# Moving GpSimd's share of the lo parts, quarters and sums of squares to VectorE, and starting the feed-forward with four weight groups

## The chip, the core and the metric

One core of a Trainium2 chip runs the whole program. The metric is device time in microseconds (us) of one execution; lower is better. The engines are TensorE (PE, with its weight loads PEld), VectorE (DVE), ScalarE (ACT), GpSimd (POOL) and SyncE (SP, which issues most transfers).

## The reference, cut to what matters

Two layers of a decoder over 1024 tokens with 1024 features. Every product is in float32.

```python
for i in range(DEPTH):                                   # 2
    proj = rmsnorm(h, attn_norm_g[i]) @ w_in[i]          # split into four head groups
    y_a = mla_group(...)      # 4 heads, causal softmax attention
    y_b = fox_group(...)      # 4 heads, causal softmax attention with a forgetting bias
    y_c = hgrn2_group(...)    # gated linear recurrence
    y_d = s5_group(...)       # complex-diagonal state space
    h = h + concat(rmsnorm of each, y_c gated) @ w_out[i]
    h = h + conv_ffn(rmsnorm(h, ffn_norm_g[i]), w_up[i], conv_w[i], conv_b[i], w_down[i])
    h = h + sigmoid(rmsnorm(h, ple_norm_g[i]) @ w_ple_gate[i]) * (p[i] @ w_ple[i])
return rmsnorm(h, final_norm_g)

def conv_ffn(x, w_up, conv_w, conv_b, w_down):           # D_FF = 2816
    up = x @ w_up                                        # 1024 x 5632
    conv = causal depthwise convolution of width 3 over the tokens
    gate, val = split(conv, 2)
    return (silu(gate) * val) @ w_down
```

## The kernel before

**Layout and precision.** Activations lie transposed: features on the 128 partitions, tokens along the row, in two halves of 512 tokens. A float32 operand is split into a rounded "hi" part (ScalarE copies it to float32r) and a "lo" part (the operand minus hi, written by `K.lo`, lines 102 and 103, on whichever engine the caller names). A product is then three matmuls, hi by hi, hi by lo and lo by hi, each 128x128 by 128x512. Line 103 is therefore the line of every lo part in the kernel.

**Planner.** The program is traced by Python generators that are woven together; a planner then lays the instructions of each engine in a fixed order, by priority (program order) and readiness, and gives tiles slots of a pool. Pool `h` has 71 slots of 128x512, pool `w` 8 of 128x1024, `wx` 6 (weights split into hi and lo), `wr` 2 (raw weights).

**Attention.** `attention` (line 1026) runs eight heads, one after the other, with the next head's maxima (`Head.max`) and preparation beside it. `Head.out` (line 978) makes for each block of 128 keys the logits `qk`, two exponentials on ScalarE (`ph` rounded, `pr` full), the lo part `pl` on GpSimd, every fourth on VectorE (line 1013), and three block products behind the three matmuls of `pv` into `po`, which needs `pl`. `Head.max` ends in three instructions of eight columns on VectorE (`mr`, `mm`, lines 944 to 946), whose result TensorE transposes (`pm`, line 952) before the next head's logits can start. A head has two accumulations `po`, one for each half of the queries; 96 `pl` in a layer.

**Norms.** `Norm.square` (line 805) squares a tile on ScalarE and adds it into one of two sums, even tiles on `engs[0]` (VectorE), odd ones on `engs[1]` (GpSimd), line 814. `rms_steps` (line 844) normalises, rounds and writes lo parts alternately by VectorE and GpSimd (line 863).

**Feed-forward, first product.** `ffn_up` (line 1304) computes blocks of two by two quarters by seven half-sized products (Strassen's scheme in Winograd's form). The input's eight quarter tiles are built by `Quarters`: `left` (line 1259) normalises the first half of the tokens and gives the operands of products 1 and 2; `right` (line 1266) normalises the second half, forms the sums and differences, and gives those of 6, 5, 7, 3 and 4, in that order. Of its work, lo parts of odd tiles and two kinds of subtractions (lines 1285 and 1294) are GpSimd's. For each of 22 weight groups, `raw` loads four quarters of weights, `piece` makes the hi and lo of a product's weights (`wx`), and `step` runs the product (12 matmuls, lines 1356 to 1358) and adds its result up on VectorE; after product 3 and after product 4 a convolution follows (lines 1366 to 1368). The order is products 1, 2, 6, 5, 7, 3, 4 (`SEQ`); groups 0 and 1 go through it together, from group 2 on one group after the other. Pieces are made five products ahead (`up=5`). Pieces of products 1, 2 and 4 have their lo part on GpSimd, others on VectorE. Beside `left` and `right`, `embed` runs the products `pw` of the layer's embedding.

The residual `h` lies in the eight slots of pool `w` until `right` has read it.

Of the kernel before, what the change touches and what calls it, by code (L numbers as in the profile page):

```python
# [14 lines left out]
ALU = mybir.AluOpType  # L15
# [8 lines left out]
KD = D // P  # L24
DEPTH = 2
NFF = 22
# [12 lines left out]

T = dict(early=(0, 0.2), s5=((0.1, 0.7), (0.1, 0.7)), hgrn=((0.2, 0.92), (0.2, 0.92)), cd=((0.05, 0.85), (0.05, 0.85)), prep=((0.3, 1), (0.3, 1)), b=(0, 1), a=(0.9, 0.95), pre=(8, 10, 12, 13), vals=(5, 6), ahead=3, plv=4, mx=8, pw=1, rt=2, sc=2, rp=6, dl=4, qk=(4, 4), up=5)


class Kern:
# [733 lines left out]
class Norm:  # L779


    def __init__(self, K, gains, width, split=True, engs=None, pairs=0):

        self.pairs = pairs
        self.K, self.gains, self.width, self.split = K, gains, width, split
        k = width // P
        self.engs = engs or (K.nc.vector, K.nc.gpsimd)
        self.xs = [[None, None] for _ in range(k)]
        self.acc, self.r_, self.last = [[None, None], [None, None]], [None, None], None

# [53 lines left out]
def rms_steps(K, tiles, gains, out, gates=None):  # L844

    nc = K.nc
    V = nc.vector
    new = [[] for _ in tiles]
    out.extend(new)
    nm = Norm(K, gains, P * len(tiles), split=False)  # L850
    for n in range(2):
        for i, x in enumerate(tiles):
            nm.add(i, n, x[n])
        yield
        nm.scale(n)
        yield
        for i, x in enumerate(tiles):
            xn, hi, lo = K.h(name="xn"), K.h(F32R, "yh"), K.h(F32R, "yl")
            V.scalar_tensor_tensor(xn, x[n], gains[:, i:i + 1], nm.r(n), op0=ALU.mult, op1=ALU.mult)
            if gates is not None:  # L860
                V.tensor_tensor(xn, xn, gates[i][n], op=ALU.mult)
            nc.scalar.copy(hi, xn)
            K.lo(V if i % 2 else nc.gpsimd, lo, xn, hi)
            new[i].append((hi, lo))
        yield

# [38 lines left out]
class Head:  # L905
# [69 lines left out]

    def out(self, ahead=T['ahead']):

        K, nc = self.K, self.K.nc
        V = nc.vector
        po = {}  # L980

        def pv(qh, kt, n, ph, pl):
            if kt == 0:
                po[qh] = K.po()
            o = po[qh][:, HS - n:HS]
            vh, vl = (t[:, kt % 4, :] for t in self.v[kt // 4])
            last = kt == 4 * qh + 3
            nc.tensor.matmul(o, lhsT=vh, rhs=ph[:, 0:n], start=(kt == 0), stop=False)
            nc.tensor.matmul(o, lhsT=vh, rhs=pl[:, 0:n], start=False, stop=False)
            nc.tensor.matmul(o, lhsT=vl, rhs=ph[:, 0:n], start=False, stop=last)  # L990
            if last:
                vs, os_ = slice(self.vo, self.vo + 64), slice(self.oo, self.oo + 64)
                r = K.h(name="ri")
                nc.scalar.activation(r[vs, :], po[qh][os_, :], AF.Ln)
                nc.scalar.activation(r[vs, :], r[vs, :], AF.Exp, scale=-1.0)
                V.tensor_tensor(self.y[qh][vs, :], po[qh][vs, :], r[vs, :], op=ALU.mult)
                self.half = qh + 1

        pend = []
        for qh, kt in [(0, kt) for kt in range(4)] + [(1, kt) for kt in range(8)]:  # L1000
            diag = kt >= 4 * qh
            q0 = (kt - 4 * qh) * P if diag else 0
            n = HS - q0
            ps = K.px("qk")
            for j, (kk, qq, nr) in enumerate(self.passes):
                nc.tensor.matmul(ps[:, 0:n], lhsT=kk[kt // 4][0:nr, (kt % 4) * P:(kt % 4 + 1) * P],
                                 rhs=qq[qh][0:nr, q0:HS], start=(j == 0), stop=(j == len(self.passes) - 1 and not diag))
            if diag:
                nc.tensor.matmul(ps[:, 0:P], lhsT=K.mk, rhs=K.identb, start=False, stop=True)
            pr, ph, pl = K.h(name="pr"), K.h(F32R, "ph"), K.h(F32R, "pl")  # L1010
            nc.scalar.activation(ph[:, 0:n], ps[:, 0:n], AF.Exp)
            nc.scalar.activation(pr[:, 0:n], ps[:, 0:n], AF.Exp)  # L1012
            K.lo(V if T['plv'] and kt % T['plv'] == T['plv'] - 1 else nc.gpsimd, pl[:, 0:n], pr[:, 0:n], ph[:, 0:n])
            pend.append((qh, kt, n, ph, pl))
            if len(pend) > ahead:
                pv(*pend.pop(0))
            yield
        while pend:
            pv(*pend.pop(0))
            yield  # L1020
# [203 lines left out]
class Quarters:  # L1224
# [34 lines left out]
    def left(self, h):  # L1259

        for m in range(KD):
            self.norm(m, 0, h[m][0])
            self.split(1 if m < KD // 2 else 2, self.q[m][0], self.K.nc.gpsimd if m % 3 == 2 else None)
            yield

    def right(self, h):

        V, G = self.K.nc.vector, self.K.nc.gpsimd
        H = KD // 2
        q, t2 = self.q, []  # L1270
        for k in range(H):
            self.norm(k, 1, h[k][1])
            self.norm(H + k, 1, h[H + k][1])
            t = self.K.h(name="t2")
            t2.append(t)
            V.tensor_tensor(q[k][0], q[k][1], q[k][0], op=ALU.subtract)
            V.tensor_tensor(t, q[H + k][1], q[k][0], op=ALU.subtract)
            self.split(6, t)
            yield
        for k in range(H):  # L1280
            self.split(5, q[k][0])
            if k % 2:
                yield
        for k in range(H):
            G.tensor_tensor(q[k][1], q[H + k][1], q[k][1], op=ALU.subtract)
            self.split(7, q[k][1], G if k % 2 else V)
            if k % 2:
                yield
        for k in range(H):
            self.split(3, q[H + k][1], G if k % 2 else V)  # L1290
            if k % 2:
                yield
        for k in range(H):
            G.tensor_tensor(q[H + k][0], q[H + k][0], t2[k], op=ALU.subtract)
            self.split(4, q[H + k][0], G if k % 2 else V)
            if k % 2:
                yield
        self.flush()


SEQ = (1, 2, 6, 5, 7, 3, 4)


def ffn_up(K, xq, h, w_up, vec, hid, beside, down):
# [6 lines left out]
    nc = K.nc  # L1311
    V, G = nc.vector, nc.gpsimd
    HV = (slice(0, HS), slice(HS, S))
    first = lambda g: (g // 2) * 2 + (NFF if g % 2 else 0)
    groups = [dict(f=first(g)) for g in range(NFF)]
    order = [(g, p) for p in SEQ for g in range(2)] + [(g, p) for g in range(2, NFF) for p in SEQ]

    def raw(g):

        q = groups[g]  # L1320
        r = K.sp.tile([P, S], F32, name=K._nm("wr"), tag="wr", bufs=2)
        q["a"] = [r[:, HV[0]], r[:, HV[1]], K.h(name="wq"), K.h(name="wq")]
        for i, t in enumerate(q["a"]):
            nc.sync.dma_start(t, w_up[q["f"] + i // 2][:, HV[i % 2]])

    def piece(g, p):

        q = groups[g]
        if "a" not in q:
            raw(g)  # L1330
        a11, a12, a21, a22 = q["a"]
        eng = V
        if p == 6:
            q["s1"], q["s2"] = K.h(name="s1"), K.h(name="s2")
            V.tensor_tensor(q["s1"], a21, a22, op=ALU.add)
            V.tensor_tensor(q["s2"], q["s1"], a11, op=ALU.subtract)  # L1336
            x = q["s2"]
        elif p == 5:
            x = q["s1"]
        elif p == 7:  # L1340
            V.tensor_tensor(a21, a11, a21, op=ALU.subtract)
            x = a21
        elif p == 3:
            V.tensor_tensor(a12, a12, q["s2"], op=ALU.subtract)
            x = a12
        else:
            x, eng = {1: a11, 2: a12, 4: a22}[p], G
        t = q["w", p] = K.wx()
        nc.scalar.copy(t[:, HV[0]], x)  # L1349
        K.lo(eng, t[:, HV[1]], x, t[:, HV[0]])  # L1350
# [58 lines left out]
    def parts():  # L1409
        nonlocal at  # L1410
        left = xq.left(h)
        for i in range(KD):
            yield next(left)
            if i == T['sc']:
                xq.nm.scale(1)
        piece(*order[0])
        piece(*order[1])
        for _ in range(T['rp']):
            yield next(right)
        piece(*order[2])  # L1420
        piece(*order[3])
        at = 4

    weave((beside, 2 * KD, 0, T['pw']), (parts(), 8 + T['rp']))
# [178 lines left out]
def body(ctx, tc, xT, pT, pos, invf, sgn, vecs, prms, dsk, bfs, w_fm, w_misc, w_tm, w_uq, w_ukv, w_glu,  # L1603
         w_outb, w_up, w_down, w_pg, w_ple, out):
    nc = tc.nc
# [66 lines left out]
    for l in range(DEPTH):  # L1672
# [184 lines left out]
        def embed_load():  # L1857
            for i in range(2):
                for n in range(2):
                    p_, a, b = praw[i][n], K.h(F32R, "ph"), K.h(F32R, "pl")  # L1860
                    nc.scalar.copy(a, p_)
                    K.lo(nc.gpsimd, b, p_, a)
                    pp[i].append((a, b))

        def embed():
# [187 lines left out]
```

## Time and profile before

| | us |
|---|---|
| median of 3 runs | 2956.09 |
| lowest and highest of them | 2949.54, 2966.23 |
| the profiled execution's own time | 2966.12 |
| its span, first to last instruction | 2964.4 |

| stage, layer 0 | us from the span's start |
|---|---|
| input projections, state space, recurrence | 0 to 385 |
| attention, with output products beside it | 385 to 690 |
| last output product, embedding, `left` | 690 to 730 |
| first product of the feed-forward | 730 to 1170 |
| second product of the feed-forward | 1170 to 1394 |
| gate of the layer's embedding | 1394 to 1483 |

The second layer repeats this from 1483 us on; its attention lies at 1840 to 2147, its feed-forward begins at 2188. In the profile PE's busy time counts overlapping matmuls, so a stage where it reads 100% has no waits, but a smaller share still tells how much waiting there was. A wait is put down to the instruction that released it last.

### The profile page before, as it was taken

How to read it: one execution, taken by the hardware profiler on the slowest of the kernel's cores; microseconds unless marked ns; L12 is line 12 of the kernel's file. 1: busy time of each engine (PE TensorE's matmuls, PEld its weight loads, DVE VectorE, ACT ScalarE, POOL GpSimd, SP SyncE). 2: the span in 40 equal slices, each digit the busy share in tenths (PEclk: the TensorE clock that was granted, in tenths of full speed). 3: DMA queues.
4: the chain of work that ended last, by engine and by line, in shares of the span. 5: the costliest groups of instructions: out<-in, count | busy, mean ns of one | idle time of the engine just before them, and what ended most of it. 6: DMA issues, size and time to landing. Idle time of an engine off the chain costs nothing. (4 is left out here: it accounts for less than half of the span.)

```text
span 2964.4 us, 37115 instructions
## 1 busy us (share of the span) xinstructions
PE 2771.1 (93%) x13082; PEld 2227.8 (75%) x13082; DVE 2341.3 (79%) x3538; ACT 1460.2 (49%) x2539; POOL 813.7 (27%) x743
## 2 busy tenths in 40 slices
PE   8899899898899999999999898988989999999997
PEld 6777676666688887877887786766767888878776
DVE  7785857658999998898847776766599999989887
ACT  4234457665544444444823263666654444444455
POOL 2620113445422221003523200324453222200053
PEclk9898899999999999999998798998999999999998
DMA  3101021103222224722520011120132222264323
GB/s 128 39 23 43 22 66 39 58 8 139 71 85 84 86 86 138 260 87 89 168 70 28 20 51 39 61 62 17 40 122 78 86 81 76 85 212 171 131 84 131
DMA packets 125354, 249.36 MB, mean 84 GB/s; under 512 B 19600, under 2 KB 22288, under 8 KB 125168
## 3 DMA queue, kind: packets, MB, share of 16 engines
q1 hardware_dynamic: 123728, 246.34, 24.9%
q8 instruction: 103, 1.69, 0.2%
q10 hardware_dynamic: 1440, 0.65, 0.1%
q14 instruction: 83, 0.68, 0.1%
HBM read 191.81 MB, written 48.50 MB: 81 GB/s over the span
## 5 line engine op out<-in xcount | busy, mean ns | idle before, releaser
L1356 PE MATMUL up<-bh,wx 128*128 128x512 f32 x1232 | 481.8, 391 | 10.6 <-ACT wx L1349 10.6
L1357 PE MATMUL up<-bl,wx 128*128 128x512 f32 x1232 | 482.7, 392 | 8.1 <-DVE bl L103 4.1
L1358 PE MATMUL up<-bh,wx 128*128 128x512 f32 x1232 | 483.0, 392 | 6.3 <-DVE wx L103 6.3
L1356 PEld LDWEIGHTS up<-bh,wx 128*128 128x128 f32 x1232 | 233.1, 189 | 60.0 <-ACT wx L1349 11.5
L1357 PEld LDWEIGHTS up<-bl,wx 128*128 128x128 f32 x1232 | 233.2, 189 | 58.3 <-DVE bl L103 4.9
L1358 PEld LDWEIGHTS up<-bh,wx 128*128 128x128 f32 x1232 | 233.0, 189 | 56.6 <-DVE wx L103 8.4
L103 POOL TENSOR_TENSOR wx<-wr,wx 128x512 fp32r<-128x512 f32 (+1 forms) x117 | 225.1, 1925 | 119.2 <-ACT wx L1349 66.1
L1558 PE MATMUL dn<-g,wx 128*128 128x512 f32 x616 | 241.9, 397 | 10.9 <-DVE wx L103 10.8
L103 POOL TENSOR_TENSOR pl<-pr,ph 128x512 fp32r<-128x512 f32 x144 | 163.8, 1147 | 317.8 <-ACT pr L1012 255.1
L1557 PE MATMUL dn<-g,wx 128*128 128x512 f32 x616 | 243.1, 395 | 5.6 <-DVE g L103 5.6
L1556 PE MATMUL dn<-g,wx 128*128 128x512 f32 x616 | 238.2, 390 | 0.0
L814 POOL TENSOR_TENSOR sq<-sq,sq 128x512 f32<-128x512 f32 x52 | 91.7, 1763 | 524.2 <-ACT sq L808 522.6
L774 PE MATMUL pj<-xs,wx 128*128 128x512 f32 (+1 forms) x512 | 211.0, 412 | 13.8 <-ACT xs L801 7.2
L776 PE MATMUL pj<-xs,wx 128*128 128x512 f32 (+1 forms) x512 | 206.8, 405 | 0.7 <-DVE wx L103 0.5
L775 PE MATMUL pj<-xs,wx 128*128 128x512 f32 (+1 forms) x512 | 206.8, 404 | 0.6 <-DVE xs L802 0.6
L103 POOL TENSOR_TENSOR wx<-wq,wx 128x512 fp32r<-128x512 f32 x44 | 64.8, 1472 | 517.3 <-ACT wx L1349 517.3
L103 DVE TENSOR_TENSOR wx<-wr,wx 128x1024 fp32r<-128x1024 f32 (+2 forms) x153 | 161.3, 1055 | 46.5 <-ACT wx L750 37.0
L1367 DVE SCALAR_TENSOR_TENSOR cv<-u,vec,cv 128x1023 f32<-128x1023 f32 x88 | 131.0, 1491 | 24.9 <-ACT cv L1366 24.8
L1558 PEld LDWEIGHTS dn<-g,wx 128*128 128x128 f32 x616 | 116.7, 191 | 41.9 <-DVE wx L103 17.7
L1478 ACT CAST g<-g 128x512 fp32r<-128x512 f32 x154 | 93.4, 620 | 99.6 <-PE dn L1558 56.5
L1557 PEld LDWEIGHTS dn<-g,wx 128*128 128x128 f32 x616 | 117.6, 191 | 31.1 <-DVE g L103 6.5
L1349 ACT CAST wx<-s 128x512 fp32r<-128x512 f32 x88 | 54.1, 622 | 172.1 <-DVE s L1336 98.9
(479 smaller groups left out, 7210.4 us busy)
## 6 DMA issues: line engine op xcount, KB each, us to landing
wr<-in_w_up SPq DMA_DIRECT2D x88, 256.0 KB
wq<-in_w_up SPq DMA_DIRECT2D x88, 256.0 KB
hid<-cv SPq DMA_DIRECT2D x44, 512.0 KB
wr<-in_w_down SPq DMA_DIRECT2D x88, 256.0 KB
g<-hid SPq DMA_DIRECT2D x88, 256.0 KB
wr<-in_w_fm SPq DMA_DIRECT2D x30, 512.0 KB
wr<-in_w_pg SPq DMA_DIRECT2D x28, 512.0 KB
hdr<-h SPq DMA_DIRECT2D x48, 256.0 KB
```

The lines of the kernel that those rows point to most:

```text
L103: eng.tensor_tensor(out, x, hi.bitcast(F32), op=ALU.subtract)
L774: nc.tensor.matmul(out, lhsT=ah, rhs=bh, start=(i == 0), stop=False)
L775: nc.tensor.matmul(out, lhsT=ah, rhs=bl, start=False, stop=False)
L776: nc.tensor.matmul(out, lhsT=al, rhs=bh, start=False, stop=(i == n - 1))
L1356: nc.tensor.matmul(ps, lhsT=ah, rhs=bh, start=k == 0, stop=False)
L1357: nc.tensor.matmul(ps, lhsT=ah, rhs=bl, start=False, stop=False)
L1358: nc.tensor.matmul(ps, lhsT=al, rhs=bh, start=False, stop=k == KD // 2 - 1)
L1367: V.scalar_tensor_tensor(c[:, 1:], u[:, :S - 1], cw[:, 1:2], c[:, 1:], op0=ALU.mult, op1=ALU.add)
L1478: nc.scalar.copy(o, x)
L1556: nc.tensor.matmul(o, lhsT=ah, rhs=gh, start=f == 0, stop=False)
L1557: nc.tensor.matmul(o, lhsT=ah, rhs=gl, start=False, stop=False)
L1558: nc.tensor.matmul(o, lhsT=al, rhs=gh, start=False, stop=f == H - 1)
```

## The change

Six edits, with no change in what is computed.

1. In the feed-forward, products 1 and 2 are run for four groups (`LEAD`) before product 6 of groups 0 and 1. So eight products, not four, stand ahead of the first one that needs `right`; groups 2 and 3 later have five products each instead of seven.
2. For groups 2 and 3 the upper two weight quarters are loaded once more for this, into a tile of pool `w` (`wl`, 512 KB); their four quarters are loaded again by `raw` when their turn comes.
3. `right`'s remaining steps go on from product 4 on, not from product 2 on (`rt`).
4. All lo parts and subtractions of `Quarters` go to VectorE, and the lo parts of the pieces of products 1 and 2 for the first four groups.
5. In attention all `pl` go to VectorE (`plv` is gone).
6. `Norm` adds both sums of squares on VectorE unless told otherwise (the gate's norm still names GpSimd); the lo parts of `rms_steps` and of the embedding's input go to VectorE.

```diff
-T = dict(... ahead=3, plv=4, mx=8, pw=1, rt=2, ...)
+T = dict(... ahead=3, mx=8, pw=1, rt=4, ...)
-        self.engs = engs or (K.nc.vector, K.nc.gpsimd)
+        self.engs = engs or (K.nc.vector, K.nc.vector)
-            K.lo(V if i % 2 else nc.gpsimd, lo, xn, hi)
+            K.lo(V, lo, xn, hi)
-            K.lo(V if T['plv'] and kt % T['plv'] == T['plv'] - 1 else nc.gpsimd, pl[:, 0:n], pr[:, 0:n], ph[:, 0:n])
+            K.lo(V, pl[:, 0:n], pr[:, 0:n], ph[:, 0:n])
...
-            self.split(1 if m < KD // 2 else 2, self.q[m][0], self.K.nc.gpsimd if m % 3 == 2 else None)
+            self.split(1 if m < KD // 2 else 2, self.q[m][0])
...
-            G.tensor_tensor(q[k][1], q[H + k][1], q[k][1], op=ALU.subtract)
-            self.split(7, q[k][1], G if k % 2 else V)
+            V.tensor_tensor(q[k][1], q[H + k][1], q[k][1], op=ALU.subtract)
+            self.split(7, q[k][1])
...
-            self.split(3, q[H + k][1], G if k % 2 else V)
+            self.split(3, q[H + k][1])
...
-            G.tensor_tensor(q[H + k][0], q[H + k][0], t2[k], op=ALU.subtract)
-            self.split(4, q[H + k][0], G if k % 2 else V)
+            V.tensor_tensor(q[H + k][0], q[H + k][0], t2[k], op=ALU.subtract)
+            self.split(4, q[H + k][0])
+LEAD = 4
-    order = [(g, p) for p in SEQ for g in range(2)] + [(g, p) for g in range(2, NFF) for p in SEQ]
+    order = [(g, p) for p in SEQ[:2] for g in range(LEAD)] + [(g, p) for p in SEQ[2:] for g in range(2)]
+    order += [(g, p) for g in range(2, NFF) for p in (SEQ[2:] if g < LEAD else SEQ)]
...
-        if "a" not in q:
-            raw(g)
-        a11, a12, a21, a22 = q["a"]
+        if 2 <= g < LEAD and p < 3:
+            if "lead" not in q:
+                q["lead"] = K.wide(name="wl")
+                nc.sync.dma_start(q["lead"], w_up[q["f"]])
+            a11, a12 = q["lead"][:, HV[0]], q["lead"][:, HV[1]]
+        else:
+            if "a" not in q:
+                raw(g)
+            a11, a12, a21, a22 = q["a"]
...
-            x, eng = {1: a11, 2: a12, 4: a22}[p], G
+            x = a11 if p == 1 else a12 if p == 2 else a22
+            eng = V if g < LEAD and p < 3 else G
...
-        piece(*order[0])
-        piece(*order[1])
+        for i in range(4):
+            piece(*order[i])
         for _ in range(T['rp']):
             yield next(right)
-        piece(*order[2])
-        piece(*order[3])
         at = 4
...
-                    K.lo(nc.gpsimd, b, p_, a)
+                    K.lo(V, b, p_, a)
```

## Rows read from the trace of the kernel before

**Rows 1.** The page's head: span, and each engine's busy time.
```profile
span 2964.4 us, 37115 instructions
PE 2771.1 (93%) x13082; PEld 2227.8 (75%) x13082; DVE 2341.3 (79%) x3538; ACT 1460.2 (49%) x2539; POOL 813.7 (27%) x743
```

**Rows 2.** Engines by stage: start and end, length, busy us (instructions), clock, DMA.
```profile
core 0: us, PE busy (x) PEld busy (x) DVE busy (x) ACT busy (x) POOL busy (x), PEclk, DMA share, GB/s
690.00:740.00 50.00, 43.86 (x174) 34.15 (x173) 45.40 (x49) 26.11 (x47) 26.85 (x17) 0.94 0.44 158
740.00:800.00 60.00, 49.49 (x206) 39.35 (x204) 59.86 (x67) 31.10 (x50) 30.63 (x17) 0.94 0.16 58
...
385.00:690.00 305.00, 275.72 (x1330) 208.96 (x1329) 199.90 (x349) 195.05 (x409) 113.40 (x125) 0.97 0.15 46
...
800.00:1170.00 370.00, 370.00 (x1632) 306.48 (x1633) 337.12 (x397) 163.18 (x216) 87.68 (x55) 1.00 0.27 91
```

**Rows 3.** Waits of TensorE, 640 to 1400 us: total us, times, longest.
```profile
PE up L1356 <- ACT wx L1349: 5.3, 1, 5.3
...
PE up L1358 <- DVE wx L103: 3.2, 1, 3.2
PE up L1357 <- POOL bl L103: 2.0, 1, 2.0
PE up L1357 <- DVE bl L103: 2.0, 1, 2.0
PE ss L834 <- ACT bh L1256: 1.8, 1, 1.8
PE ob L763 <- POOL yl L103: 1.2, 1, 1.2
PE ob L762 <- ACT yh L862: 1.1, 1, 1.1
```

**Rows 4.** VectorE in order of time inside `right`: start, us, instruction.
```profile
734.09 0.68 DVE L1276 TENSOR_TENSOR xq<-xq,xq 128x512 f32<-128x512 f32 x1
734.80 0.69 DVE L1277 TENSOR_TENSOR t<-xq,xq 128x512 f32<-128x512 f32 x1
735.41 1.75 DVE L103 TENSOR_TENSOR bl<-xq,bh 128x512 fp32r<-128x512 f32 x1
```

**Rows 5.** GpSimd in order of time, the same stretch.
```profile
734.85 1.77 POOL L1285 TENSOR_TENSOR xq<-xq,xq 128x512 f32<-128x512 f32 x1 [1.89 <-DVE xq L1276]
```

**Rows 6.** VectorE in order of time, 746 to 763 us, GpSimd idle.
```profile
750.13 1.28 DVE L103 TENSOR_TENSOR bl<-xq,bh 128x512 fp32r<-128x512 f32 x2
```

**Rows 7.** GpSimd's groups by form, 700 to 800 us: busy us, mean ns.
```profile
L103 POOL TENSOR_TENSOR bl<-xq,bh 128x512 fp32r<-128x512 f32 x8 | 14.4, 1803 | 13.4 <-ACT bh L1256 10.8 <-DVE bl L103 2.4
L103 POOL TENSOR_TENSOR wx<-wr,wx 128x512 fp32r<-128x512 f32 x8 | 13.5, 1695 | 6.3 <-ACT wx L1349 6.3
L1285 POOL TENSOR_TENSOR xq<-xq,xq 128x512 f32<-128x512 f32 x4 | 7.2, 1796 | 6.9 <-DVE xq L1276 6.9
L1294 POOL TENSOR_TENSOR xq<-xq,t 128x512 f32<-128x512 f32 x4 | 6.9, 1729 | 0.0
```

**Rows 8.** Waits of TensorE in attention, 385 to 690 us.
```profile
PE pm L952 <- DVE vl L972: 6.6, 3, 3.1
PE po L989 <- POOL pl L103: 4.7, 10, 0.8
PE po L989 <- DVE pl L103: 3.6, 3, 3.1
...
PE pm L952 <- DVE mm L946: 3.4, 3, 1.2
```

**Rows 9.** One line of VectorE, all 16 heads: shortest, median, longest in ns.
```profile
L945 DVE COPY mm<-mr x16: 169/1164/1687, 422.0 to 2098.2; 128x8 f32<-128x8 f32 x16
```

**Rows 10.** The page's group of `pl` on GpSimd, both layers.
```profile
L103 POOL TENSOR_TENSOR pl<-pr,ph 128x512 fp32r<-128x512 f32 x144 | 163.8, 1147 | 317.8 <-ACT pr L1012 255.1
```

**Rows 11.** TensorE in order of time where a `pl` of VectorE was late.
```profile
496.18 0.33 PE L989 MATMUL po<-pl,vh 128*128 128x128 f32 x1 [3.14 <-DVE pl L103]
```

More of the change, by code (lines that the diff above doesn't have):

```diff
@@ L37 @@
 NS5 = 24 + 4 * 128
-T = dict(early=(0, 0.2), s5=((0.1, 0.7), (0.1, 0.7)), hgrn=((0.2, 0.92), (0.2, 0.92)), cd=((0.05, 0.85), (0.05, 0.85)), prep=((0.3, 1), (0.3, 1)), b=(0, 1), a=(0.9, 0.95), pre=(8, 10, 12, 13), vals=(5, 6), ahead=3, plv=4, mx=8, pw=1, rt=2, sc=2, rp=6, dl=4, qk=(4, 4), up=5)
+T = dict(early=(0, 0.2), s5=((0.1, 0.7), (0.1, 0.7)), hgrn=((0.2, 0.92), (0.2, 0.92)), cd=((0.05, 0.85), (0.05, 0.85)), prep=((0.3, 1), (0.3, 1)), b=(0, 1), a=(0.9, 0.95), pre=(8, 10, 12, 13), vals=(5, 6), ahead=3, mx=8, pw=1, rt=4, sc=2, rp=6, dl=4, qk=(4, 4), up=5)
 class Kern:
@@ L1262, in left @@
             self.norm(m, 0, h[m][0])
-            self.split(1 if m < KD // 2 else 2, self.q[m][0], self.K.nc.gpsimd if m % 3 == 2 else None)
+            self.split(1 if m < KD // 2 else 2, self.q[m][0])
             yield
     def right(self, h):
-        V, G = self.K.nc.vector, self.K.nc.gpsimd
+        V = self.K.nc.vector
         H = KD // 2
```

## The prediction

> **What bounds the kernel now.** I read the page's head first, then the stages, then what TensorE waits for. Over the span TensorE is busy for 93% and VectorE for 79% [rows 1], but the average hides where they meet. By stages [rows 2], the steady part of the feed-forward's first product (800 to 1170 us) has TensorE at 370.00 of 370 us: nothing can be gained there by taking work off TensorE's suppliers, and 370.00 / 1632 = 0.227 us is the pace of a matmul, so a product of 12 takes 2.72 us. VectorE runs at 337.12 of 370 us beside it, 91%. The 60 us before it are the opposite: VectorE at 59.86 of 60, TensorE at 49.49, clock 0.94. So at the head of the feed-forward VectorE is the bound and TensorE stands. In attention (385 to 690) TensorE has 275.72 of 305 and VectorE 199.90: neither is full, and chains between them decide.
>
> TensorE's waits name the places. At the feed-forward's head of layer 0 four waits of products sum to 5.3 + 3.2 + 2.0 + 2.0 = 12.5 us [rows 3]; the 5.3 is product 6, the first that needs `right`, and all four end on work that stood in VectorE's queue. Ahead of them the last output product and the norm lose 1.8 + 1.2 + 1.1 = 4.1 us. Layer 1 shows the same rows. In attention the largest are the transposes `pm`, 6.6 + 3.4 = 10.0 us in a layer, and the `pl`, 4.7 + 3.6 = 8.3 us [rows 8].
>
> **Why VectorE is full.** The same lo part takes 1.75 us while GpSimd works and 0.68 us or less else: at 735.41 it starts beside GpSimd's subtraction of 734.85 and ends with it plus its own time [rows 4, 5]; with GpSimd idle two of them take 1.28 us together, 0.60 us from start to start [rows 6]. So an instruction of GpSimd with two inputs of 512 columns costs VectorE 1.75 - 0.68 = 1.07 us when it meets one with inputs in SBUF, and would cost it 0.60 us if VectorE did it itself. This also reaches tiny instructions: the copy `mm` of eight columns takes 0.169 us at best and 1.164 in the median [rows 9].
>
> **Part 1, the quarters and the lead's pieces on VectorE.** In 700 to 800 us GpSimd does 8 lo parts of quarters, 8 of weights, and 4 + 4 subtractions [rows 7]; all 24 move. If each blocked VectorE, VectorE gains 24 x (1.07 - 0.60) = 11.3 us in that stretch. The bounds: nothing blocked, then it loses 24 x 0.60 = 14.4 us; all blocked, gain 11.3. I take near the second, 10 us, because VectorE has no idle time there [rows 2], so that nearly every instruction of GpSimd meets one.
>
> The Trainium skill (page "Perfetto Trace Analysis", section "Optimizing Scalar/DVE Operations") says that where VectorE is saturated, giving some work to ScalarE or even GpSimd may make sense, and adds that the port which the two share may spoil it. Its first half speaks against this change; it is rival D below. The durations of rows 4 to 6 bear out its second half.
>
> **Part 2, eight products ahead.** The first product that needs `right` comes four products later, 4 x 2.72 = 10.9 us. The 5.3 us wait has then 10.9 + 10 us of slack: gone. The other three (7.2 us) are VectorE's lateness further on. What is late next: with products 1 and 2 done ahead, four groups run their five heavy products back to back. A group costs VectorE 337.12 / 370 x 19.05 = 17.4 us for the 19.05 us of its seven products, nearly all of it in the five heavy ones (13.6 us of TensorE), so VectorE falls back by some 3 us a group, 12 us over four. Against that stand the light products: eight of them, 21.8 us of TensorE, ask VectorE for 8 lo parts and 4 additions, 12 x 0.60 = 7.2 us, 14.6 us free for `right`. About even, so I keep 1.5 us of waiting: 11 us a layer go. Between 690 and 800 the clock is at 0.94 [rows 2], 6.6 us; short stalls end in stretches at the lower level, and I count 2 us back with them. Sum 13 us a layer, 26 in both. Bounds: 0 and 12.5 + 6.6 = 19.
>
> The new loads are two of 512 KB in a layer. They need a slot of pool `w`, which `right` frees only at its first steps, and then 3.3 us at the 158 GB/s of that stretch [rows 2], an estimate, plus one copy and one lo part. SP's queue is passed by transfers of the embedding alone there. Nothing to pay if the planner runs products 2 of groups 0 and 1 meanwhile; 4.5 us for each load if it doesn't.
>
> **Part 3, sums of squares and lo parts of norms.** The 4.1 us ahead of the feed-forward wait for a chain with 4 instructions of GpSimd or blocked ones in it; I take half, 2 us a layer, 4 in both. Bounds 0 and 8.2. In the other stages (start, second product) the sums have no wait of over 1 us behind them: 0, bounds 3 either way. The embedding's input: 4 lo parts in a layer, 2.4 us of VectorE, hidden while TensorE runs the output products.
>
> **Part 4, attention.** GpSimd then has no instruction with inputs left there but memsets. The chain `mr`, `mm`, `mm`, `vl` ahead of `pm` shrinks: `mm` alone by 1.164 - 0.169 = 1.0 us in the median, the longest by 1.5 [rows 9], and its neighbours with it. Of the 10.0 us of `pm` I keep 2.5 for what the chain takes unblocked (some 0.3 us for each of eight heads): 7.5 us a layer, 15 in both. Bounds 0 and 20.
>
> Against it, 72 `pl` more in a layer on VectorE, at most 0.60 us each, 43 us in 305: VectorE goes from 199.90 to at most 243 us, 80%, less what is no longer blocked. No new bound. But each now queues behind maxima, preparations and weight splits, in a fixed order. Price: now 144 on GpSimd cost 4.7 us of waits in a layer [rows 8, 10], and the 24 on VectorE 3.6, of which one is 3.1 [rows 8, 11]. All 96 at VectorE's rate of 3.6 / 24 = 0.15 us make 14.4 us, 6 more than the 8.3 now; none late, 8.3 less. I take 1.5 us more a layer, 3 in both, nearer to the middle, as the late one of rows 11 stood behind work that is itself blocked less.
>
> **Sum.** -26 - 4 - 15 + 3 = -42 us. The profiled execution took 2966.1 us, so 2924 for one like it; the median of the runs is 10 us below it, so **2914 us**, 1.4% faster.
>
> **Rivals.**
> A. *VectorE stays the bound at the head.* The 12 us that four heavy groups cost VectorE come back as waits. The lead then gives 1 to 6.5 us a layer: 2927 to 2938 us. For it: 91% in the steady part; against: the 14.6 us of free time.
> B. *It comes to nothing.* The planner lays out each engine's order anew; late loads cost 2 x 4.5 = 9 us a layer, `pl` sit at their upper bound, 6 us a layer. 2956 - 42 + 18 + 9 = 2941, and with half of the `pm` gain missing 2949 us. The change would then not do what it says: product 6 would still follow a wait.
> C. *Attention pays, slower.* If `pl` is as late as in rows 11 at the end of every accumulation, two a head, 16 heads: 32 x 3.1 = 99 us, so 2956 - 45 + 99 = 3010 us. It makes the kernel slower by over 0.5% from (45 + 15) / 32 = 1.9 us for each accumulation. For it: VectorE's order is fixed, and the late one stood behind a weight split. Against: only one in a layer is so late now, and three key blocks are kept in flight.
> D. *A full VectorE only gets fuller.* The 24 moved instructions cost their 0.60 us and give nothing back: 14.4 us more waiting a layer, 2956 + 29 - 12 = 2973 us. Against: rows 4 to 6.
>
> **How the numbers follow.** Forecast 0.56, A 0.18, B 0.13, C 0.08, D 0.05. The forecast's own bounds are 2956 - 2 x (19 + 4.1 + 10 + 8.3) = 2873 at the low end; not all can go, so I end at 2880. Upwards the range takes in A and B and the lower part of C and D: 2880 to 2965. About 0.5% (15 us) is what a measurement of this kernel can tell from no change: faster is the forecast and nearly all of A (0.73), same is B and the rest of A (0.15), slower is C and D (0.12).
>
> **What would show it.** Product 6 of group 0 starts without a wait, and no lo part of `Quarters` takes over 0.8 us; VectorE's busy time in the head falls though its instructions rise; `mm` takes 0.17 us at all heads and `pm` waits under 0.5 us; attention ends some 6 us earlier after its own start. Wrong would be: waits of products 3 to 7 of groups 0 to 3 on `wx` of VectorE (A), on `wl` (B), or many waits of over 1 us on `pl` (C).

## The result, and the profile after

| | before | after |
|---|---|---|
| median of 6 runs each, us | 2960.64 (2949.54 to 2968.76) | 2929.78 (2927.05 to 2939.45) |
| ratio after / before, 95% interval | | 0.990 (0.988 to 0.993) |
| profiled execution, its span, us | 2966.12, 2964.4 | 2929.51, 2927.8 |

The change makes the kernel 1.0% faster: 31 us between the medians, 36.6 us between the profiled spans. The forecast was 42 us and 2914. One of e1's five runs below took 9310.32 us: e1's ratio leaves it out, its median counts it.

The page's head of after, with the group of `pl` (busy us, mean ns, then idle time before it):

```profile
span 2927.8 us, 36891 instructions
PE 2760.6 (94%) x13082; PEld 2218.8 (76%) x13082; DVE 2356.8 (80%) x3792; ACT 1460.2 (50%) x2539; POOL 466.5 (16%) x489
...
L103 DVE TENSOR_TENSOR pl<-pr,ph 128x512 fp32r<-128x512 f32 x192 | 105.6, 555 | 38.6 <-ACT pr L1012 36.5
```

Against [rows 1], 254 instructions went from GpSimd to VectorE. GpSimd lost 347.2 us of busy time by it, VectorE gained 15.5 us, 0.06 us for each. A moved lo part takes VectorE 0.56 us in the mean (`pl` above) or 0.69 us (512 columns), so most of what it took on it got back from instructions no longer held up. For TensorE, 2964.4 - 2771.1 = 193.3 us of idle time became 167.2: 26.1 of the 36.6 us are shorter waits, the other 10.5 us are the same 13082 matmuls taking less time. That goes with the granted clock, whose mean over the span is 0.955 before and 0.959 after (by it some 13 us less are lost against a full clock).

To see where, I cut each layer at TensorE's own instructions. **Attention** runs from the first matmul of `lg` (the logits from which the maxima are taken) to the last of `po`, the **tail** from there to the first `pw`, the **head and first product** from the first `pw` to the last `up`. The windows of TensorE between those points, attention in both layers, before (length, busy us of each engine, then clock):

```profile
411.70:679.10 267.40, 239.81 (x1178) 180.94 (x1179) 174.33 (x315) 174.47 (x374) 102.80 (x115) 0.96 0.10 30
1867.30:2136.50 269.20, 243.09 (x1178) 183.07 (x1179) 174.78 (x311) 174.46 (x374) 102.17 (x115) 0.94 0.10 30
```

and after:

```profile
409.90:668.30 258.40, 242.99 (x1188) 183.68 (x1188) 195.64 (x397) 174.47 (x374) 12.55 (x36) 0.95 0.11 33
1850.10:2103.10 253.00, 237.23 (x1187) 179.48 (x1188) 195.17 (x393) 174.21 (x374) 12.55 (x36) 0.98 0.11 33
```

Length less PE busy is TensorE's idle time: 27.6 and 26.1 us before, 15.4 and 15.8 after. The same reading of every kernel, both layers with a comma between (length / idle us / clock; of the tail the length):

| kernel | attention | tail | head and first product | span |
|---|---|---|---|---|
| before | 267.4/27.6/.96, 269.2/26.1/.94 | 29.5, 29.4 | 460.8/14.3/.99, 463.5/14.3/.98 | 2964.4 |
| after | 258.4/15.4/.95, 253.0/15.8/.98 | 29.5, 29.6 | 454.9/10.9/.99, 455.6/10.0/.99 | 2927.8 |
| e1: `pl` alone | 258.1/15.0/.94, 257.0/15.0/.95 | 27.0, 27.0 | 462.3/15.1/.99, 462.3/15.1/.99 | 2942.3 |
| e2: all but `pl` | 276.2/26.0/.92, 275.7/28.7/.93 | 30.8, 30.8 | 454.3/10.2/1.00, 456.2/10.6/.99 | 2961.5 |
| e8: GpSimd reads again | 281.5/33.5/.95, 281.2/33.6/.95 | 29.7, 29.7 | 455.6/10.0/.99, 456.7/10.1/.99 | 2976.3 |
| e9: GpSimd fills | 261.8/14.8/.93, 254.5/15.1/.97 | 29.5, 29.6 | 454.5/10.2/.99, 456.4/10.0/.99 | 2929.7 |
| e5: pieces after `right` | 260.1/14.9/.94, 262.4/14.8/.93 | 29.7, 29.5 | 453.6/9.1/.99, 453.1/8.2/.99 | 2931.0 |
| e6: two groups ahead | 257.5/15.4/.95, 256.4/15.1/.96 | 29.5, 29.6 | 448.0/4.5/1.00, 447.9/4.5/1.00 | 2910.3 |
| e12: four, no new load | 260.1/15.2/.94, 254.0/16.6/.98 | 29.7, 29.6 | 447.2/3.9/1.00, 447.2/3.9/1.00 | 2910.0 |
| e7: embedding's lo parts back | 263.3/16.5/.94, 256.6/15.4/.96 | 28.0, 28.0 | 458.1/10.7/.99, 456.9/9.9/.99 | 2936.8 |
| e10: norms' share back | 255.3/16.6/.96, 254.1/15.4/.96 | 27.0, 27.7 | 457.0/9.6/.99, 456.4/9.4/.99 | 2918.2 |
| e11: e6 and e10 | 253.8/15.9/.97, 256.7/14.7/.95 | 27.0, 26.9 | 448.2/4.4/1.00, 448.8/4.0/.99 | 2904.2 |

The idle columns hardly move between kernels with the same code in a stage; lengths move by up to 9 us with the clock. So effects are read from idle time, and a few microseconds of length in attention are no evidence.

Of the 36.6 us, attention gives 9.0 + 16.2 = 25.2 (22.5 of it idle time), the head 5.9 + 7.9 = 13.8 (7.7 idle), the tail -0.2, the rest -2.2. The stages ahead of attention (411.7 and 385.0 us before) and the second product (224.1 and 222.8) move by at most 4.8 us, in both directions.

**The head**, which answers to [rows 2]:

```profile
core 0: us, PE busy (x) PEld busy (x) DVE busy (x) ACT busy (x) POOL busy (x), PEclk, DMA share, GB/s
690.00:740.00 50.00, 42.17 (x175) 32.91 (x174) 39.64 (x63) 27.15 (x50) 0.00 (x0) 0.93 0.47 169
740.00:800.00 60.00, 60.00 (x266) 49.72 (x265) 59.73 (x87) 31.00 (x47) 7.04 (x4) 1.00 0.22 76
```

VectorE's busy time over the two falls from 105.26 to 99.37 us though it has 34 instructions more, and TensorE fills the second to 60.00 at clock 1.00. But in the first window VectorE, full before, now idles 10 us and TensorE 8. TensorE's waits from 640 to 1380 us, against [rows 3]:

```profile
PE pw L762 <- ACT pw L1882: 6.1, 1, 6.1
PE dn L1567 <- DVE wx L103: 4.3, 4, 1.5
PE up L1367 <- ACT wx L1360: 3.3, 2, 3.1
PE ob L762 <- ACT yh L862: 3.3, 1, 3.3
PE ob L762 <- DVE h L1815: 3.0, 2, 1.7
...
PE ss L834 <- DVE sq L826: 1.7, 2, 1.4
```

The four waits of products (12.5 us) are down to 3.3, and product 6 starts without one. Two rows are new or larger: `pw`, a product of the embedding that waits for ScalarE, and `ob`, the output products at the end of attention, 6.3 us against 1.1 + 1.2 + 0.7 (the 0.7 on `h` isn't shown in [rows 3]). What stood in front of `pw` is in ScalarE's order of time (in brackets the idle time before):

```profile
715.50 0.59 ACT L1882 COPY pw<-pw 128x512 f32<-128x512 f32 x1 [0.26 <-PE pw L764]
724.09 0.62 ACT L1360 CAST wx<-wl 128x512 fp32r<-128x512 f32 x1 [8.01 <-DMA wl<-in_w_up]
725.37 0.62 ACT L1360 CAST wx<-wl 128x512 fp32r<-128x512 f32 x1 [0.66 <-DMA wl<-in_w_up]
725.89 0.61 ACT L1256 CAST bh<-t 128x512 fp32r<-128x512 f32 x1
726.41 0.58 ACT L1882 COPY pw<-pw 128x512 f32<-128x512 f32 x1
```

with the loads as SyncE issued them, and VectorE's group of the same weights, whose idle time is in the last column:

```profile
715.16 1.39 SPq L1327 DMA_DIRECT2D wq<-in_w_up  x3
716.64 0.86 SPq L1337 DMA_DIRECT2D wl<-in_w_up  x2
...
L103 DVE TENSOR_TENSOR wx<-wl,wx 128x512 fp32r<-128x512 f32 x4 | 2.8, 688 | 7.2 <-ACT wx L1360 7.2
```

ScalarE works in a fixed order. The two new loads `wl` (512 KB each) are issued at 716.64, right behind quarters `wq` of groups 0 and 1, and the first can be copied only at 724.09. That copy stands ahead of copies that empty `pw`; ScalarE idles 8.01 us on it, VectorE 7.2 on ScalarE's result, TensorE 6.1 on `pw`. Layer 1 has the same row, 5.2 us.

**Attention** against [rows 8] and [rows 9]: TensorE's waits from 409.9 to 668.4 us, then the line of `mm` over all 16 heads (shortest/median/longest, ns).

```profile
PE po L989 <- DVE pl L103: 4.2, 5, 2.9
PE po L988 <- ACT ph L1011: 2.5, 2, 2.3
PE po L988 <- POOL vh L966: 1.4, 1, 1.4
PE lg L929 <- DVE mx L933: 1.3, 2, 0.8
...
L945 DVE COPY mm<-mr x16: 167/169/172, 418.8 to 2070.7; 128x8 f32<-128x8 f32 x16
```

The 10.0 us of `pm` are gone, the 8.3 us of `pl` are down to 4.2, and `mm` takes 0.17 us at every head.

### The profile page after: what moved, and what is told of

The parts are those of the page before. It is cut to its first block, busy times and chain, and to the rows that moved or that the text cites. A ratio compares the mean times of both kernels' runs of the same rounds, so it can differ in the third digit from the quotient of the medians.

```text
span 2927.8 us, 36891 instructions
## 1 busy us (share of the span) xinstructions
PE 2760.6 (94%) x13082; PEld 2218.8 (76%) x13082; DVE 2356.8 (80%) x3792; ACT 1460.2 (50%) x2539; POOL 466.5 (16%) x489
## 5 line engine op out<-in xcount | busy, mean ns | idle before, releaser
L103 POOL TENSOR_TENSOR wx<-wr,wx 128x512 fp32r<-128x512 f32 (+1 forms) x101 | 198.1, 1964 | 581.6 <-DVE wx L750 496.4
L1367 PEld LDWEIGHTS up<-bh,wx 128*128 128x128 f32 x1232 | 231.8, 188 | 58.4 <-ACT wx L1360 10.4
L103 DVE TENSOR_TENSOR wx<-wr,wx 128x1024 fp32r<-128x1024 f32 (+1 forms) x161 | 165.8, 1033 | 38.3 <-ACT wx L750 27.8
L1567 PEld LDWEIGHTS dn<-g,wx 128*128 128x128 f32 x616 | 116.1, 190 | 42.0 <-DVE wx L103 18.2
L1566 PEld LDWEIGHTS dn<-g,wx 128*128 128x128 f32 x616 | 117.1, 190 | 31.4 <-DVE g L103 7.2
L103 DVE TENSOR_TENSOR pl<-pr,ph 128x512 fp32r<-128x512 f32 x192 | 105.6, 555 | 38.6 <-ACT pr L1012 36.5
L1565 PEld LDWEIGHTS dn<-g,wx 128*128 128x128 f32 x616 | 116.0, 188 | 25.0 <-ACT g L1487 0.8
L1379 DVE SCALAR_TENSOR_TENSOR cv<-u,vec,cv 128x1022 f32<-128x1022 f32 x88 | 133.7, 1521 | 0.1
```

The lines of the kernel that those rows point to most:

```text
L103: eng.tensor_tensor(out, x, hi.bitcast(F32), op=ALU.subtract)
L1367: nc.tensor.matmul(ps, lhsT=ah, rhs=bh, start=k == 0, stop=False)
L1379: V.scalar_tensor_tensor(c[:, 2:], u[:, :S - 2], cw[:, 0:1], c[:, 2:], op0=ALU.mult, op1=ALU.add)
L1565: nc.tensor.matmul(o, lhsT=ah, rhs=gh, start=f == 0, stop=False)
L1566: nc.tensor.matmul(o, lhsT=ah, rhs=gl, start=False, stop=False)
L1567: nc.tensor.matmul(o, lhsT=al, rhs=gh, start=False, stop=f == H - 1)
```

## The experiments

All ratios are to the kernel before, run on the same chip, with a 95% interval. The experiments ran on three chips, on which the kernel before has medians of 2961.88 (e1 to e4), 2961.63 (e5, e6, e7, e10) and 2966.31 us (e8, e9, e11, e12), so times of runs on different chips are compared through these. Where there is one run, there is no interval.

### e1 and e2: the attention edit alone, and all but it

e1 is the kernel before with one line changed:

```diff
-            K.lo(V if T['plv'] and kt % T['plv'] == T['plv'] - 1 else nc.gpsimd, pl[:, 0:n], pr[:, 0:n], ph[:, 0:n])
+            K.lo(V, pl[:, 0:n], pr[:, 0:n], ph[:, 0:n])
```

> The kernel before with one edit: all lo parts pl of attention on VectorE. Attention, from the first product for the maxima to the last product behind po, takes 267.4 us in layer 0 and 269.2 in layer 1 before, 258.4 and 253.0 after the whole change. Theory (GpSimd blocks VectorE's instructions with inputs in SBUF): 258 and 253 within 3 us, the waits of pm gone, the head of the feed-forward as before (461 and 464 us from the first pw to the last up), 2960 - 25 = 2935 us. Rival (attention's gain came from the lo parts of the norms, or from the planner's new order): attention within 4 us of 267 and 269, time within 0.3% of before.

Measured: 2943.49 us, ratio 0.992 (0.989 to 0.995). Attention idles 15.0 us in both layers, the head is where it was. Its waits of products from 640 to 1400 us are those of [rows 3]:

```profile
PE up L1356 <- ACT wx L1349: 6.9, 1, 6.9
...
PE up L1358 <- DVE wx L103: 3.2, 1, 3.2
PE up L1357 <- DVE bl L103: 2.0, 1, 2.0
```

One edit of six gives over half of the gain, and all that attention gains in idle time: 12.6 and 11.1 us. It is slower than the 2935 us expected; in layer 1 attention takes 257.0 us, outside the 3 us around 253, at a clock of 0.95 where after had 0.98.

e2 is the kernel after with three of four `pl` on GpSimd again:

```diff
-            K.lo(V, pl[:, 0:n], pr[:, 0:n], ph[:, 0:n])
+            K.lo(V if kt % 4 == 3 else nc.gpsimd, pl[:, 0:n], pr[:, 0:n], ph[:, 0:n])
```

> The changed kernel with that one edit undone: three of four pl are GpSimd's again. Theory: attention back at 266 to 270 us in both layers, pm waits of some 8 us a layer back, head of the feed-forward as in the changed kernel (455 and 456 us), 2930 + 20 to 25 = 2950 to 2955 us. Rival: attention stays at 258 and 253, 2930 us.

Measured: 2966.11 us, ratio 1.002 (1.000 to 1.003), slower than expected. The head keeps its gain; `mm` has a mean of 1.045 us again. Attention is 8.8 and 6.5 us longer than before:

```profile
406.80:683.00 276.20, 250.21 (x1180) 187.32 (x1181) 179.27 (x323) 175.05 (x374) 91.69 (x108) 0.92 0.10 29
1864.90:2140.60 275.70, 246.96 (x1181) 185.65 (x1181) 179.37 (x319) 174.84 (x374) 91.00 (x108) 0.93 0.10 29
```

Its idle time is 26.0 and 28.7 us, that of before. What grew is the busy time of the same matmuls, by 10.4 and 3.9 us, at a clock of 0.92 and 0.93 instead of 0.96 and 0.94. Much of the loss lies in one place: from 520 to 590 us the clock is 0.90 before and 0.76 in e2, with TensorE busy for 60.47 and 62.33 us (after: 0.83 and 61.45). Why this order of work is granted less there stays open; the waits don't show it. So by waits e2 keeps the head's gain, and the clock in attention hides it.

### e3, e4, e8 and e9: is it GpSimd's reading that costs?

Theory: GpSimd's instructions with two inputs hold up VectorE's. Rival: the gain came from something else, as the GpSimd queue that `po` waited for. e3 lets GpSimd do its old subtraction again on top, into a tile that nobody reads; e4 puts fills in its place, which read nothing.

```diff
             K.lo(V, pl[:, 0:n], pr[:, 0:n], ph[:, 0:n])
+            if kt % 4 != 3:                                       # e3
+                m = min(n, 384)
+                K.lo(nc.gpsimd, K.ghost[:, 0:m], pr[:, 0:m], ph[:, 0:m])
+            if kt % 4 != 3:                                       # e4, instead
+                for _ in range(2):
+                    nc.gpsimd.memset(K.ghost[:, 0:min(n, 384)], 0.0)
```

> The changed kernel, and GpSimd does three of four subtractions once more (at most 384 columns) into a tile that nobody reads. Nothing waits for them, so only what they do to others is seen. Theory (GpSimd's reads block VectorE): the copy mm goes from 0.17 to over 0.9 us in most heads, pm waits are back, attention longer by 6 us or more a layer (264 and 259). Rival (what was dear was the latency of GpSimd's own pl in front of the products behind it): attention at 258 and 253 within 2 us.

> As the kernel with the second subtraction, but GpSimd fills that tile twice with zeros instead, so it is about as busy and reads nothing from SBUF. Theory (it is the reading of inputs that blocks): mm stays at 0.17 us, attention at 258 and 253 within 2 us. Rival (any work of GpSimd blocks VectorE): like the other kernel, 264 and 259.

e3: 2972.26 us in one run, attention 280.3 and 279.8 us, idle 33.0 and 31.8. In attention all of the gain is gone and more (27.6 and 26.1 us idle before). `mm` rose only to a mean of 0.444 us, not over 0.9 as expected: the `pl` themselves, now at VectorE, were what was held up most. e4: 2955.72 in one run, and no answer. The fills wait for nothing, so the planner put them into the stage ahead of attention:

```profile
0.00:430.00 430.00, 370.44 (x1985) 294.94 (x1986) 290.85 (x654) 160.79 (x310) 188.28 (x432) 0.88 0.16 55
430.00:692.00 262.00, 247.09 (x1196) 186.84 (x1195) 197.07 (x399) 176.18 (x377) 12.54 (x36) 0.94 0.11 33
```

GpSimd (fifth column) is busy for 188.28 us ahead and for 12.54 us in attention. So e8 and e9 repeat the pair with the tile `pr` itself as target, which ties both to their place behind `pl`:

```diff
             K.lo(V, pl[:, 0:n], pr[:, 0:n], ph[:, 0:n])
+            if kt % 4 != 3:                                       # e8
+                K.lo(nc.gpsimd, pr[:, 0:n], pr[:, 0:n], ph[:, 0:n])
+            if kt % 4 != 3:                                       # e9, instead
+                for _ in range(2):
+                    nc.gpsimd.memset(pr[:, 0:n], 0.0)
```

> The changed kernel; behind three of four pl GpSimd does the same subtraction once more into pr, which nobody reads after it. It starts when VectorE's pl is done, so it delays nothing but what it blocks. Theory (GpSimd's reads of SBUF block VectorE): attention 264 us and 259 us or more instead of 258.4 and 253.0. Rival (blocking is harmless where pl itself is not GpSimd's): within 2 us of these.

> As the kernel that reads again behind pl, but GpSimd fills pr twice with zeros, which reads nothing, at the same places and for about the same time. Theory (it is the reading that blocks): within 2 us of 258.4 and 253.0. Rival (any work of GpSimd, or pr's slot held longer, is what costs): as long as the kernel that reads again.

e8: 2978.05 us, e9: 2931.4 us, a run each. VectorE's groups of `pl` (410 to 680 us) and TensorE's waits in attention of layer 0, first e8:

```profile
L103 DVE TENSOR_TENSOR pl<-pr,ph 128x384 fp32r<-128x384 f32 x15 | 14.7, 982 | 1.6 <-ACT pr L1012 1.4
L103 DVE TENSOR_TENSOR pl<-pr,ph 128x128 fp32r<-128x128 f32 x15 | 8.4, 558 | 1.0 <-ACT pr L1012 0.7
...
PE po L989 <- DVE pl L103: 10.8, 13, 4.5
PE po L988 <- ACT ph L1011: 4.7, 4, 2.3
PE pm L952 <- DVE mm L946: 4.6, 5, 1.9
```

and e9:

```profile
L103 DVE TENSOR_TENSOR pl<-pr,ph 128x384 fp32r<-128x384 f32 x16 | 8.9, 554 | 0.7 <-ACT pr L1012 0.6
L103 DVE TENSOR_TENSOR pl<-pr,ph 128x128 fp32r<-128x128 f32 x16 | 4.6, 287 | 2.3 <-ACT pr L1012 1.9
...
PE po L989 <- DVE pl L103: 4.0, 4, 3.0
```

With GpSimd busy for 99.4 us, most of it reading, VectorE's lo part of 384 columns takes 0.98 us, `pm` waits are back and TensorE idles 33.5 us. With 75.5 us of filling at the same places it takes 0.55 us, as in after, and the idle time is after's (14.8 against 15.4). So GpSimd's two-input subtraction costs, its fill doesn't; that it is the reading follows as far as reading is what sets the two apart. By length e9's attention is 3.4 us over after's in layer 0, at a clock of 0.93 against 0.95, outside the 2 us expected. Two things the pair doesn't show. The eight-column copy `mm` has nearly the same mean in both, 0.298 us beside reads and 0.277 beside fills (0.169 in after), so that reading alone holds it up isn't shown; its longest differ, 1.225 and 0.452 us, and only e8 has `pm` waits. And the fills are 24 us shorter, so they also hold `pr` for less.

### e5, e6 and e12: what the lead is worth, and what the late load costs

e5 emits the pieces of groups 2 and 3 behind `right`'s first six steps, as a repair of the 6.1 us wait:

```diff
-        for i in range(4):
+        for i in range(2):
             piece(*order[i])
         for _ in range(T['rp']):
             yield next(right)
+        for i in range(2, 4):
+            piece(*order[i])
```

> The changed kernel with one edit: the pieces of groups 2 and 3 for product 1 come behind right's first six steps, not ahead of them, in the order in which the planner sees them. In the changed kernel ScalarE stands 8.0 us at the copy of the late weights wl, and the copies of pw queue behind it, so TensorE waits 6.1 and 5.2 us for pw. Theory (a queue behind a late load): that wait goes, first pw to last up takes 449 and 450 us instead of 455 and 456, 2930 - 12 = 2918 us. Rival (the loads themselves are too late): products 1 of groups 2 and 3 wait 5 us and more instead, 455 and 456 us, 2930 us.

Measured: 2923.44 us, ratio 0.987 (0.985 to 0.990), but not by the repair: ScalarE still stands 7.7 us before the copy of `wl`, and TensorE 5.9 us before `pw`. The head idles 1.8 us a layer less; the longest wait of a product, 3.1 us in after, is 1.1 here. On the whole e5's interval overlaps that of after. ScalarE's waits from 700 to 740 us:

```profile
ACT wx L1360 <- DMA wl<-in_w_up: 8.4, 2, 7.7
```

The planner put the copies in the same place; the order in the source didn't decide. e6 takes the lead away: two groups, as before, with the quarters and the pieces on VectorE. e12 keeps four groups without a new load: groups 2 and 3 take products 1 and 2 from the weights of groups 0 and 1, which changes what those two groups compute, not how much work they are, but for the load.

```diff
-LEAD = 4                                                          # e6, with rt=2 and e5's edit
+LEAD = 2
-                q["lead"] = K.wide(name="wl")                     # e12
-                nc.sync.dma_start(q["lead"], w_up[q["f"]])
-            a11, a12 = q["lead"][:, HV[0]], q["lead"][:, HV[1]]
+                q["lead"] = groups[g - 2]["a"][:2]
+            a11, a12 = q["lead"]
```

> The changed kernel with two groups ahead, the old order of products and pieces and the old start of right's last steps; quarters and pieces stay on VectorE, nothing is loaded twice. Theory 1 (the work on VectorE alone was enough): no product waits over 1.5 us, first pw to last up in 447 to 450 us, 2930 - 14 = 2916 us. Theory 2 (eight products ahead were needed): product 6 waits 3 us or more, 455 us or more, 2930 us or more.

> The changed kernel with four groups ahead but without the extra load: groups 2 and 3 take their products 1 and 2 from the weights of groups 0 and 1, so that part of the result is another; the amount of work is the same but for two loads of 512 KB a layer. Theory (the late load and the queue behind it cost what four groups gain): no wait of pw over 1.5 us, first pw to last up 446 to 449 us instead of 455 and 456. Rival (four heavy groups in a row cost it): 453 us or more.

e6: 2918.74 us, ratio 0.986 (0.984 to 0.988); e12: 2911.67 in one run. The head idles 4.5 us in each layer of e6 and 3.9 us in each of e12, instead of 10.9 and 10.0 in after, at a clock of 1.00. TensorE's waits of products from 690 to 1160 us, in e6:

```profile
PE up L1367 <- ACT wx L1360: 3.1, 1, 3.1
```

and in e12:

```profile
PE up L1366 <- ACT wx L1359: 1.5, 2, 1.1
...
PE up L1368 <- DVE wx L103: 0.6, 2, 0.4
```

In e6 one product still waits over 1.5 us, against what its Theory 1 said; the length and the time are Theory 1's. The head and first product of layer 0, first before, then e6:

```profile
708.60:1169.40 460.80, 446.51 (x1947) 367.13 (x1946) 427.74 (x492) 210.00 (x296) 137.06 (x84) 0.99 0.27 92
694.20:1142.20 448.00, 443.53 (x1946) 365.78 (x1946) 417.11 (x514) 211.03 (x297) 101.56 (x62) 1.00 0.27 95
```

VectorE has 22 instructions more, GpSimd 22 fewer, and VectorE's busy time falls by 10.6 us. So moving the work to VectorE, without the lead, takes the head from 460.8 to 448.0 us (e6); `pl` and the norms have no share in it, as e1 (462.3) and e11 (448.2) show. Products of two more groups ahead add 0.8 and 0.7 us (e12 against e6). Their load, with what queues behind it, costs 454.9 - 447.2 = 7.7 and 8.4 us a layer (after against e12).

### e7, e10 and e11: the norms' share, and the best of the parts

```diff
-                    K.lo(V, b, p_, a)                             # e7, e10, e11
+                    K.lo(nc.gpsimd, b, p_, a)
-        self.engs = engs or (K.nc.vector, K.nc.vector)            # e10, e11
+        self.engs = engs or (K.nc.vector, K.nc.gpsimd)
-            K.lo(V, lo, xn, hi)                                   # e10, e11
+            K.lo(V if i % 2 else nc.gpsimd, lo, xn, hi)
```

e11 has e6's edit too.

> The changed kernel with only the four lo parts of the embedding's input in a layer back on GpSimd. Theory (in VectorE's queue they stand ahead of the additions to h and of the last norm, and so make the last output product wait): last po to first pw 27 us instead of 29.5, the waits of ob down by 3 us. Rival (the norm's own lo parts or sums do it): 29.5 us stay.

> The changed kernel with the sums of squares, the lo parts of the norms and of the embedding's input back on GpSimd as before. Theory (these moves cost more at the end of attention than they give): last po to first pw in 27.0 us instead of 29.5, as in the kernel with pl alone, attention as in the changed kernel, 2930 - 5 = 2925 us. Rival (they are needed, GpSimd's few reads block again): attention longer by 4 us a layer, 2938 us.

> Two groups ahead as before the change, and norms and embedding's input back on GpSimd; pl, quarters and the first pieces of products 1 and 2 on VectorE. If the two undone parts are independent: first pw to last up 448 us, last po to first pw 27 us, 2919 - 5 = 2914 us. Rival (in that stretch VectorE's gain is used up once GpSimd reads again): head 452 us, 2922 us.

e7: 2938.56 us in one run, within the range of after's runs; its tail is 28.0 us, not the 27 expected. e10: 2925.18, ratio 0.987 (0.985 to 0.989), tail 27.0 and 27.7. e11: 2910.45, ratio **0.982 (0.980 to 0.984)**, tail 27.0 and 26.9; it beats both kernels. TensorE's waits for the last output products in e10, from 655 to 830 us:

```profile
PE pw L762 <- ACT pw L1882: 5.5, 1, 5.5
...
PE ob L763 <- POOL yl L103: 1.7, 1, 1.7
PE ob L762 <- DVE h L1815: 1.3, 2, 1.0
```

The 6.3 us of `ob` in after are 3.0 here. With the norms' share at GpSimd the tail is 2.5 and 1.9 us shorter than in after; of that 1.5 us come with the embedding's four lo parts alone (e7). The `pw` wait of the late load is untouched, as it should be, and goes only with e6's edit.

## Why the prediction came out as it did

**Direction and mechanism held.** "Why VectorE is full" was right. In the head VectorE's lo parts of `bl` take 0.687 us on average with none over 0.70, where one had taken 1.75 beside GpSimd [rows 4]; in attention e8 against e9 shows that GpSimd's two-input work costs what its fills don't. Rival D, that a full VectorE only gets fuller, did not come true: in the first 110 us of the head 34 instructions more took VectorE 5.9 us less. The Trainium skill (page "Perfetto Trace Analysis", section "Optimizing Scalar/DVE Operations") says that work may go from a saturated VectorE to GpSimd, and warns that the read port which the two share may make that useless. The trace agrees with the warning: beside a full VectorE these instructions were cheaper on VectorE itself. In the head no run parts two causes, VectorE no longer held up and lo parts that come sooner (0.687 us where GpSimd's took 1.80 [rows 7]); the fall of VectorE's busy time shows the first, the share of the second stays open.

**Part 1 held.** The price of 1.07 against 0.60 us, a gain of 0.47 us for each moved instruction, carried: in e6, which has little but this in the head, 22 moved ones took 10.6 us off VectorE, 0.48 us each. TensorE's head became 12.8 us shorter in layer 0, about the 13 us a layer that the forecast gave to Parts 1 and 2 together.

**Part 2 failed at "nothing to pay if the planner runs products 2 of groups 0 and 1 meanwhile".** What covered TensorE was asked; who stands behind the load's consumer wasn't. The copy of `wl` sits in ScalarE's fixed order ahead of copies that other products need. The first load, put at 3.3 us, took 7.4 from its issue to its use; in SyncE's queue it stood behind quarters `wq` too, not behind transfers of the embedding alone. Rival B's price, 4.5 us for each of two loads, was nearly what e12 shows (7.7 and 8.4 us a layer for the pair), and it should have been a term of the sum. The credit to eight products was wrong as well: with VectorE relieved, two groups give all but 0.8 us. Lead: 26 us forecast, 13.8 measured. Of the clock's 2 us a layer the trace shows 3 in layer 0: from 690 to 800 us 6.6 us were lost at 0.94, now it is 3.5, all of it at 0.93 in the first 50.

**Rival A** happened once a layer: product 7 of a later group waits 3.1 us (820.73 us) for VectorE, which is at convolutions. Its 12 us didn't come.

**Part 3 failed at "hidden while TensorE runs the output products".** The embedding's lo parts stand in VectorE's queue ahead of the additions to `h` and the last norm; `ob` waits grew by 3.3 us. Tail: a gain of 2 us a layer forecast, none measured (29.5 and 29.6 us). By idle time it got worse, 6.3 and 6.9 us against 3.9 before, though the tail has 8 and 7 matmuls fewer (attention has 10 and 9 more).

**Part 4 was mis-sized, and one sign was wrong.** `pm` fell by all of its 10.0 us, not 7.5: the 2.5 us kept for the unblocked chain cost TensorE nothing. `pl` was priced at +1.5 us a layer, "nearer to the middle", and came out at 4.2 - 8.3 = -4.1 in layer 0. The late 3.14 us of [rows 11] survives (2.9), but the ten waits on GpSimd's `pl` went. (The 144 `pl` of [rows 10] are those of both layers, the 4.7 us of [rows 8] of one; the sum didn't use that price.) For 512 columns GpSimd took 1.29 us in attention of layer 0 and VectorE takes 0.69 in after, so a `pl` can be ready sooner even behind a queue; the wait in the queue itself was not measured.

```profile
L103 POOL TENSOR_TENSOR pl<-pr,ph 128x512 fp32r<-128x512 f32 x40 | 51.5, 1291 | 147.3 <-ACT pr L1012 119.1 <-PE qk L1009 16.9 <-PE lg L932 7.1
L103 DVE TENSOR_TENSOR pl<-pr,ph 128x512 fp32r<-128x512 f32 x48 | 33.1, 690 | 17.6 <-ACT pr L1012 17.2
```

Attention: 12 us forecast, 25.2 measured, 22.5 of them idle time. Rival C's queue didn't build up: VectorE is at 195.64 of 258.4 us.

**The sum** of -42 stands near -36.6 by luck, because the errors of the parts had opposite signs: 12 us too much for the lead, 4 for the tail, 13 too little for attention, 2 in the rest. The base was the other miss. I took the median of runs 10 us below the profiled execution; after's median equals its profiled execution (2929.78 and 2929.51), and before's, over six runs, is 5.5 us below its own. So of the 16 us between 2914 and 2929.78, 5 come from the terms and 10 from that step.

**Open.** What decides the clock in attention (0.92 to 0.98 with the same matmuls, 5 to 22 us a layer) and ahead of it (0.89 to 0.91 in layer 1) isn't settled. Nor was a later place for the `wl` load tried, since e6 and e12 say it could give 0.8 us at most over e6.

## What to carry to other kernels

Price an instruction on a second engine by what it does to the first one's neighbours, and look at the shortest instructions of the critical chain: here the chain of an eight-column copy held up by 1 us cost TensorE 10.0 us a layer, more than the 8.3 us that it waited for the `pl`, most of which moved. For every new load, follow each in-order queue that its consumer sits in, and ask what else waits behind it there. When a change has several parts, run each alone: here the four groups, one of the two parts in the title, cost 7 us a layer, and the kernel without them and without the norms' edit (e11) gains 1.8% instead of 1.0%.

## What the hardware showed that I had not expected

GpSimd's fills didn't hold up VectorE's two-input instructions of 128 to 512 columns (0.554 us for 384 columns beside 75.5 us of GpSimd's fills and in after, 0.982 where it reads), but the copy `mm` of eight columns rose beside them from 0.169 to 0.277 us in the mean. VectorE's maxima of logits (`mx`, 512 columns, read from where TensorE put them) took 0.686 us both beside GpSimd's subtractions and without them, in before and after. The granted clock alone moved attention by up to 10 us at equal idle time, so two kernels that differ by less than that there can't be told apart by length. The first of two loads of 512 KB, issued right behind four of 256 KB, was there for use 7.4 us after its issue.
